# Attention products of a two-block transformer as plain float32 matmuls on halves of the array

## The chip, the core and the metric

The kernel runs on one core of a Trainium2 chip. TensorE multiplies matrices: a stationary operand of up to 128 rows by 128 columns is loaded, and a moving operand of up to 512 columns runs through it into a bank of PSUM. VectorE, ScalarE and GpSimd (POOL in the profile) do everything else, and SyncE starts the transfers from main memory. The metric is the device time of one execution in microseconds (us), as the median of several runs.

## What is computed

Two blocks of two layers each on 256 tokens of width 1024, all in float32. Each layer has a mixing part and a gated feed-forward part (FFN), and there is one FFN more ahead of the mixing part in the second block. The second block puts 16 meta tokens ahead of the 256. Cut to the attention parts, which are all that the change touches:

```python
def memory_cross_attention(q, mem_k, mem_v):              # 4 heads of 64, layers 0 and 1
    s = einsum("bshd,bmhd->bhsm", q, mem_k) * 64**-0.5
    return einsum("bhsm,bmhd->bshd", softmax(s), mem_v)

def stick_breaking_attention(q, k, v):                    # 12 heads of 64, layer 1
    z = einsum("bhtd,bhsd->bhts", qb, kb) * scale         # causal, blocks of 128 queries
    log_not = where(causal, log_sigmoid(-z), 0.0)
    a = where(causal, exp(log_sigmoid(z) + reverse_cumsum(log_not) - log_not), 0.0)
    out = einsum("bhts,bhsd->bhtd", a, vb)

def _diff_attention(...):                                 # 8 heads, each two maps of width 64, values of 128
    logits = einsum("bqhmd,bkhmd->bmhqk", qb, k) * scale + bias
    p = softmax(where(visible, logits, NEG_INF))
    out = einsum("bhqk,bkhe->bqhe", p[:, 0] - lam_full * p[:, 1], v)

def _dsa_attention(...):                                  # 16 heads over one latent of 256; 8 index heads of 64
    act = relu(einsum("bqhd,bsd->bqhs", qi, k_idx) * 64**-0.5)
    score = einsum("bqh,bqhs->bqs", wi, act)              # the 64 best keys of each query are kept
    logits = einsum("bqhr,bqkr->bqhk", qa, kv) * 256**-0.5 + bias
    o_lat = einsum("bqhk,bqkr->bqhr", softmax(logits), kv)
    out = einsum("bqhr,hrd->bqhd", o_lat, w_uv)
```

The kernel multiplies latent and `w_uv` first and so has values of width 64 per head in the last one.

## The kernel before

Activations lie feature by token: 8 tiles of 128 features by 256 (or, with the meta tokens, 272) tokens. Weights stream from main memory in pieces of 128 x 1024 words. Each piece is split in two on the way: ScalarE copies it to the shorter format float32r (`wh`, line 187), VectorE, for some pieces POOL, takes the difference (`wl`, line 189). Activations are split likewise by `split_act` and `split_scaled` (lines 216 to 223). A product of two split operands is three float32r matmuls, `mm3`: high by high, high by low, low by high (lines 212 to 214). The trace names these lines for nearly all of TensorE's work, in the attention as in the dense layers, so tiles tell the places apart: `z` and `s` are PSUM banks of scores, `o` of outputs, `mm` of dense products, `t`, `b` and `n` of transposes and norms.

The order of the work is not the code's. A scheduler reads the program, with the functions' calls as its order of preference, and moves instructions of each engine where data and buffers allow; it often puts the matmuls of one score between those of a dense product.

The stages in order of time: mix0 (gated convolution, and memory attention in `mem_pair`), FFN 0, mix1 (stick-breaking attention in `pair`, and `mem_pair`), FFNs 1 and 2, diff (`diff_mix`), FFNs 3 and 4, dsa (`dsa_mix`), FFN 5. How the attention parts use the array before:

- Scores with heads of 64 features (`mem_pair`, `pair`, the diff scores, dsa's index scores) have 64 rows of the array, the lower ones for even heads, the upper ones for odd heads; one head's three matmuls stand together in the code, with all 128 columns.
- Values for two heads of 64 (`mem_pair`, `pair`, dsa's `apply_v`) are loaded together as 128 columns, and each head's probabilities run through both. Half of what comes out is not used: `pair_out` picks rows 0 to 63 of the first head's 256 columns and rows 64 to 127 of the second's (line 551).
- In diff and dsa the probabilities of 256 queries over the keys are transposed by TensorE to four tiles of 128 columns (`probs_t`), split, and multiplied in four parts: 256 columns, 128 columns, and twice 128 columns for the meta positions, which have 48 rows only (`K = slice(0, 48)`, line 1027).
- dsa's scores have 256 features, two full tiles of rows (line 1229).
- dsa's search for the 64 best keys (`top_rounds`, 8 rounds on VectorE for each of two halves of the queries) follows the index scores; the first attention heads need its mask.

PSUM has eight banks. The kernel gives them to tags: `banks(mm=3, z=3, o=2)` in the first block and in all FFNs, other shares in diff and dsa.

Of the kernel before, what the change touches and what calls it, by code (L numbers as in the profile page):

```python
# [6 lines left out]
F32 = mybir.dt.float32  # L7
F32R = mybir.dt.float32r
# [21 lines left out]
HUGE = 3e38  # L30
TOPK = 64
# [99 lines left out]
class Net:  # L131
# [181 lines left out]
    def token_major(self, name, x, rc, dst):  # L313

        ws = [self.take(name, 4) for _ in range(2)]
        for tt in range(2):
# [5 lines left out]
            vh, vl = dst(tt)  # L322
            self.split_scaled(vh, vl, b[:, :S], rc[:, tt : tt + 1])
# [149 lines left out]
    def mem_side(self, i, mx, r_row, r_col, pk, tag):  # L473

        nc = self.nc
        kh = self.t(pk, [P, 2, S], tag + "kh", F32R)
        kl = self.t(pk, [P, 2, S], tag + "kl", F32R)
        banks = self.dense(f"mkv{i}", mx, S)
        for m in range(2):
            t = self.t(self.p_ev, [P, T], "ea")[:, :S]  # L480
            nc.vector.scalar_tensor_tensor(t, banks[m][:, :S], 0.125, r_row, ALU.mult, ALU.mult)
            self.split_act(kh[:, m], kl[:, m], t)
        self.ahead()
        vh = self.t(pk, [P, 2, S], tag + "vh", F32R)
        vl = self.t(pk, [P, 2, S], tag + "vl", F32R)
        self.token_major(f"mkv{i}", mx, r_col, lambda tt: (vh[:, tt], vl[:, tt]))
        self.ahead()
        return (kh, kl), (vh, vl)

    def pad_pairs(self, vh, vl, src, col, rows=P):  # L490

        s4 = src.rearrange("p (a e d) -> p a e d", e=2, d=64)
        for e in range(2):
            o = slice(192 * e, 192 * e + 64)
            if col is None:
                self.split_act(vh[:, :, o], vl[:, :, o], s4[:, :, e])
            else:
                self.split_scaled(vh[:, :, o], vl[:, :, o], s4[:, :, e], col)
# [8 lines left out]
    def mem_pair(self, qm, mk, mv, p, y, pt, nb=2):  # L507
# [3 lines left out]
        for e in range(2):  # L511
            rows = slice(e * 64, e * 64 + 64)
            s = self.bank("z")
# [21 lines left out]
            ph = self.t(pt, [P, 2, S], "th", F32R, bufs=nb)  # L535
            pl = self.t(pt, [P, 2, S], "tl", F32R, bufs=nb)
            self.split_act(ph, pl, b3)
# [889 lines left out]
```

## Time and profile before

| | |
|---|---|
| median of 3 runs | 1754.85 us (1753.32 to 1756.73) |
| profiled execution, its own time | 1751.51 us |
| its span, first to last instruction | 1749.8 us |
| TensorE busy | 1719.7 us, 13786 matmuls recorded |
| VectorE, ScalarE, POOL busy | 1165.5, 929.9, 435.5 us |
| mean granted clock of TensorE | 0.989 of full |

Busy time of an engine is the time in which at least one of its instructions runs. Matmuls are pipelined: one is recorded as running for some 0.28 us, while the next starts 0.12 us later. So the distance between two starts tells what a matmul takes of the queue, and the duration does not. Weight loads have records of their own (PEld) and run beside the matmuls. Where a row lists busy times by stretch, the order is TensorE, its weight loads, VectorE, ScalarE, POOL, with the number of instructions in brackets. The chain that ended last is followed back from the last instruction, at each step to what released it.

### The profile page before, as it was taken

To read this page: it belongs to the slowest core of one execution; us is meant where nothing else is said; L and a number is where in the kernel's file an instruction comes from. 1 tells how busy PE (TensorE), PEld (TensorE's weight loads), DVE (VectorE), ACT (ScalarE), POOL (GpSimd) and SP (SyncE) were. 2 spreads that over 40 slices of the span, in tenths; PEclk is the share of its full clock that TensorE was granted. 3 is DMA by queue.
4 is the path that set the end of the run, shared out by engine and by line. 5 is a ranking of instruction groups with operands and counts; after the bars stand their busy time and mean duration, and the time that the engine had idled before them with its cause. 6 is when DMAs were issued, how large, how long until landed. Compare 5 with 4: busy or idle time off the path is not lost.

```text
span 1749.8 us, 33756 instructions
## 1 busy us (share of the span) xinstructions
PE 1719.7 (98%) x13786; PEld 1687.2 (96%) x13786; DVE 1165.5 (67%) x1942; ACT 929.9 (53%) x1631; POOL 435.5 (25%) x450
## 2 busy tenths in 40 slices
PE   8999999999999999999999999999999989999999
PEld 7999999999999999999998999999999979999999
DVE  8867666677766666655978666556665587766653
ACT  6545445586544654444665544445444467655442
POOL 2023221013322022211443522111221234342210
PEclk9999999999999999999998999999999999999999
DMA  7456655423555545445531444444445433245552
GB/s 274 156 196 219 231 184 181 170 93 121 193 193 181 183 167 193 169 170 185 162 106 61 161 177 169 170 184 177 170 169 176 135 97 113 73 164 184 180 197 91
DMA packets 59931, 287.61 MB, mean 164 GB/s; under 512 B 12112, under 2 KB 22864, under 8 KB 29184
## 3 DMA queue, kind: packets, MB, share of 16 engines
q1 hardware_dynamic: 58944, 284.80, 46.6%
q8 instruction: 108, 1.77, 0.4%
q10 hardware_dynamic: 832, 0.66, 0.1%
q14 instruction: 47, 0.39, 0.1%
HBM read 284.34 MB, written 5.53 MB: 166 GB/s over the span
## 4 chain that ended last, share of the span: by engine, by line
PE 93%; DVE 5%; ACT 1%; DMA 1%; issue 0%; POOL 0%; ACTq 0%; DVEq 0%; POOLq 0%; SPq 0%
PE mm L212 21%; PE mm L214 21%; PE mm L213 21%; PE z L212 8%; PE z L213 8%; PE z L214 7%; DVE xl L223 1%; PE o L212 1%; PE o L213 1%; PE o L214 1%; PE s L212 1%; PE s L213 1%; PE s L214 1%; DMA X<-in_xT_dram 1%; DVE wl L189 1%
## 5 line engine op out<-in xcount | busy, mean ns | idle before, releaser
L187 ACT CAST wh<-raw 128x1024 fp32r<-128x1024 f32 (+1 forms) x526 | 541.7, 1032 | 606.8 <-PE mm L213 397.0
L189 DVE TENSOR_TENSOR wl<-raw,wh 128x1024 fp32r<-128x1024 f32 (+2 forms) x494 | 603.2, 1223 | 291.5 <-ACT wh L187 289.4
L212 PE MATMUL mm<-xh,wh 128*128 128x256 f32 (+1 forms) x1808 | 521.7, 289 | 1.5 <-DVE ea L703 0.6
L213 PE MATMUL mm<-xl,wh 128*128 128x256 f32 (+1 forms) x1808 | 518.1, 287 | 4.7 <-DVE xl L223 4.5
L214 PE MATMUL mm<-xh,wl 128*128 128x256 f32 (+1 forms) x1808 | 518.2, 287 | 0.0
L213 PEld LDWEIGHTS mm<-xl,wh 128*128 128x128 f32 x1808 | 341.4, 189 | 7.5 <-DVE xl L223 5.9
L212 PEld LDWEIGHTS mm<-xh,wh 128*128 128x128 f32 x1808 | 341.7, 189 | 5.0 <-DVE ea L703 0.9
L214 PEld LDWEIGHTS mm<-xh,wl 128*128 128x128 f32 x1808 | 342.0, 189 | 1.3 <-issue 0.2
L213 PE MATMUL z<-xl,wh 128*128 128x256 f32 (+1 forms) x1056 | 301.6, 286 | 1.5 <-DVE xl L223 1.3
L214 PE MATMUL z<-xh,wl 128*128 128x256 f32 (+1 forms) x1056 | 302.3, 286 | 0.0
L212 PE MATMUL z<-xh,wh 128*128 128x256 f32 (+1 forms) x1056 | 301.2, 285 | 0.0
L212 PE MATMUL mm<-gh,wh 128*128 128x256 f32 (+1 forms) x1056 | 300.5, 285 | 0.0
L214 PE MATMUL mm<-gh,wl 128*128 128x256 f32 (+1 forms) x1056 | 299.5, 284 | 0.0
L213 PE MATMUL mm<-gl,wh 128*128 128x256 f32 (+1 forms) x1056 | 299.5, 284 | 0.0
L339 POOL TENSOR_TENSOR es<-es,r 128x256 f32<-128x256 f32 (+1 forms) x110 | 152.3, 1387 | 466.8 <-ACT es L338 466.8
L213 PEld LDWEIGHTS z<-xl,wh 128*128 128x128 f32 x1056 | 199.2, 189 | 1.9 <-DVE xl L223 1.9
L214 PEld LDWEIGHTS z<-xh,wl 128*128 128x128 f32 x1056 | 199.8, 189 | 0.2
L212 PEld LDWEIGHTS z<-xh,wh 128*128 128x128 f32 x1056 | 199.5, 189 | 0.1
L213 PEld LDWEIGHTS mm<-gl,wh 128*128 128x128 f32 x1056 | 199.2, 189 | 0.0
L214 PEld LDWEIGHTS mm<-gh,wl 128*128 128x128 f32 x1056 | 198.5, 188 | 0.0
L212 PEld LDWEIGHTS mm<-gh,wh 128*128 128x128 f32 x1056 | 198.3, 188 | 0.0
L340 DVE TENSOR_TENSOR ea<-z,es 128x256 f32<-128x256 f32 (+1 forms) x132 | 57.1, 432 | 96.7 <-POOL es L339 48.9
(487 smaller groups left out, 2241.0 us busy)
## 6 DMA issues: line engine op xcount, KB each, us to landing
raw<-in_gu_dram SPq DMA_DIRECT2D x132, 1024.0 KB, 4.8
raw<-in_wd_dram SPq DMA_DIRECT2D x66, 1024.0 KB, 4.8
raw<-in_aw_dram SPq DMA_DIRECT2D x12, 1024.0 KB, 4.8
raw<-in_a_in_dram SPq DMA_DIRECT2D x9, 1024.0 KB, 4.9
raw<-in_wo_dram SPq DMA_DIRECT2D x12, 768.0 KB, 4.2
nb<-scr SPq DMA_DIRECT2D x32, 136.0 KB, 2.3
scr<-relrow SPq DMA_DIRECT2D x16, 271.5 KB, 5.4
raw<-in_mkv_dram SPq DMA_DIRECT2D x4, 1024.0 KB, 5.4
```

Of the source, the lines that this page charges most:

```text
L187: self.nc.scalar.copy(h[:, :c], t[:, x : x + c])
L189: eng.tensor_tensor(l[:, :c], t[:, x : x + c], h[:, :c].bitcast(F32), ALU.subtract)
L212: mm(out, wh, xh, start=first, stop=False, skip_group_check=chk)
L213: mm(out, wh, xl, start=False, stop=False, skip_group_check=chk)
L214: mm(out, wl, xh, start=False, stop=last, skip_group_check=chk)
L223: self.nc.vector.scalar_tensor_tensor(l, src, col, h.bitcast(F32), ALU.mult, ALU.subtract)
L339: nc.gpsimd.tensor_tensor(s, s, r, ALU.mult)
L340: nc.vector.tensor_tensor(a, B[:, :cols], s, ALU.mult)
```

## The change

All products inside the attention become plain float32 matmuls on unsplit operands. Queries, keys, values and probabilities are kept as one float32 tile each, so the copies to float32r become plain copies or go, and the subtractions on VectorE go. Products of dense layers, also those that make queries, keys and values, stay as they are.

Where a head has 64 features, a new helper `both` writes two heads turn by turn: the scores of one on the upper 64 rows of the array, of the other on the lower. Values of two heads are no longer loaded together: each head has 64 columns of the array, the two halves again turn by turn, and both outputs land in the same 256 columns of the bank, on rows 0 to 63 and 64 to 127; `pair_out` is one split instead of two. The meta positions' value tiles are filled with zeros to 128 rows. In mix1 the banks are shared out as mm=2, z=4, o=2. In dsa the value product is written once per two heads. In diff the norm's factor is multiplied in while queries and keys are scaled, on VectorE, instead of by POOL ahead.

```diff
+HALF = [slice(0, 64), slice(64, P)]
...
+    def both(self, jobs, start, stop):
+        for out, w, x in jobs[::-1]:
+            self.nc.tensor.matmul(out, w, x, start=start, stop=stop, skip_group_check=True)
...
@@ mem_pair @@
-            for tt in range(2):
-                c = slice(tt * P, (tt + 1) * P)
-                self.mm3(
-                    s[:, tt * S : (tt + 1) * S], (qm[0][rows, p, c], qm[1][rows, p, c]),
-                    (mk[0][rows, p], mk[1][rows, p]), True, True,
-                )
+        ss = [self.bank("z") for _ in range(2)]
+        for tt in range(2):
+            c = slice(tt * P, (tt + 1) * P)
+            self.both([(s[:, tt * S : (tt + 1) * S], qm[r, p, c], mk[r, p]) for s, r in zip(ss, HALF)], True, True)
...
-            self.split_act(ph, pl, b3)
+            nc.scalar.copy(pr, b3)
...
-                self.mm3(o[:, e * S : (e + 1) * S], v, (ph[:, kt], pl[:, kt]), kt == 0, kt == 1)
+            self.both([(o[r, :S], mv[:, kt, p * P + r.start : p * P + r.stop], pr[:, kt]) for r, pr in zip(HALF, ps)],
+                      kt == 0, kt == 1)
...
@@ pair_out @@
-        for e in range(2):
-            r = slice(64 * e, 64 * e + 64)
-            self.split_act(y[0][r, k, :S], y[1][r, k, :S], o[r, e * S : (e + 1) * S])
+        self.split_act(y[0][:, k, :S], y[1][:, k, :S], o[:, :S])
...
@@ block1_mix1 @@
+        self.banks(mm=2, z=4, o=2)
...
+                zs = [self.bank("z") for _ in range(2)]
+                self.both([(z[:, :S], k[r, p, :P], q[r]) for z, r in zip(zs, HALF)], True, False)
+                self.both([(z[:, S:NC], k[r, p, P:], q[r, P:]) for z, r in zip(zs, HALF)], False, False)
...
-                    self.split_act(ah, al, av)
...
+                self.both([(o[r, :S], v[:, 0, p, r], av[:, :S]) for r, av in zip(HALF, avs)], True, False)
+                self.both([(o[r, P:S], v[:, 1, p, r], av[:, S:]) for r, av in zip(HALF, avs)], False, True)
...
@@ diff_mix @@
+            vm = self.t(p1, [P, NH, P], "vm")
+            vn = [self.t(p1, [P, P], f"vn{i}") for i in range(LAG + 1)]
...
-                nc.gpsimd.tensor_tensor(x, x, u, ALU.mult)
...
-                    self.split_scaled(qk[0][:, i, P:], qk[1][:, i, P:], x[:, i], g)
+                    nc.vector.scalar_tensor_tensor(qk[:, i, P:], x[:, i], g, u[:, i], ALU.mult, ALU.mult)
...
+                for qc, k0, n, c, tt in SEGS:
+                    self.both([(s[:, c], qk[r, 0, P + NM + qc.start : P + NM + qc.stop], qk[r, 1, k0 : k0 + n])
+                               for s, r in zip(ss, HALF)], True, True)
...
-                self.apply_v(os[0], e, (ph, pl), lambda i: tuple(v[:, i] for v in vr),
-                             tuple(v[:, h] for v in vm), vq)
+                for i, (oc, pc, v) in enumerate(self.v_parts(vr, vm[:, h], vq)):
+                    nc.tensor.matmul(os[0][:, e * S + oc.start : e * S + oc.stop], v, pr[:, pc],
+                                     start=e == 0 and i == 0, stop=e == 1 and i == 3, skip_group_check=True)
...
@@ dsa_mix @@
-                self.split_act(qi[0][:, m], qi[1][:, m], b[:, :S])
+                nc.scalar.copy(qi[:, m], b[:, :S])
...
-                        self.mm3(s[:, c], (q[0][:, k, qc], q[1][:, k, qc]),
-                                 (ckg[0][:, k, k0 : k0 + n], ckg[1][:, k, k0 : k0 + n]), k == 0, k == 1)
+                        nc.tensor.matmul(s[:, c], q[:, k, qc], ckg[:, k, k0 : k0 + n], start=k == 0, stop=k == 1)
...
+                    for n, two_ in enumerate(zip(*parts)):
+                        self.both([(o[r, oc], w, ps[i][:, pc]) for i, (r, (oc, pc, w)) in enumerate(zip(HALF, two_))],
+                                  n == 0, n == 3)
```

On TensorE, in dsa, the value product of a second head. Before, a head's four parts are three matmuls each; `v0h` and `v0l` are the halves of the values, `ph` and `pl` of the probabilities, and the last number is output rows x columns. The first row is the end of a dense product, then come the parts of 256 and of 128 columns:

```order
L214 MATMUL mm_17462<-wh_17168,ckvl_16675 48x256
L212 MATMUL o_17431<-ph_17552,v0h_17085 128x256
L213 MATMUL o_17431<-pl_17553,v0h_17085 128x256
L214 MATMUL o_17431<-ph_17552,v0l_17086 128x256
L212 MATMUL o_17431<-ph_17552,v0h_17085 128x128
L213 MATMUL o_17431<-pl_17553,v0h_17085 128x128
L214 MATMUL o_17431<-ph_17552,v0l_17086 128x128
```

The next six rows are two more such threes, on 48 rows of the array. After, the same place for both heads of the pair, `pr_16989` and `pr_16924` their probabilities:

```order
L1179 MATMUL s_17042<-ckg_16080,q_16732 128x272 x2
L222 MATMUL o_16991<-pr_16989,v_2357_16444 64x256
L222 MATMUL o_16991<-pr_16924,v_2357_16444 64x256
L222 MATMUL o_16991<-pr_16989,v_2357_16444 64x128
L222 MATMUL o_16991<-pr_16924,v_2357_16444 64x128
```

Two more pairs of 64x128 follow. The two heads' products stand turn by turn, each on 64 columns, and nothing on 48 rows stands among them.

On TensorE, in diff, before: one head's value product behind the last row of the next head's scores (`s`, on 64 rows). The last six rows, `vmh` to `vn1l`, are on 48 rows, and the row behind them is a transpose on all rows:

```order
L214 MATMUL s_10778<-qkh_10508,qkl_10509 16x16
L213 MATMUL o_10403<-pl_10604,vh_10551 128x256
L214 MATMUL o_10403<-ph_10603,vl_10552 128x256
L212 MATMUL o_10403<-ph_10603,vh_10551 128x128
L213 MATMUL o_10403<-pl_10604,vh_10551 128x128
L214 MATMUL o_10403<-ph_10603,vl_10552 128x128
L212 MATMUL o_10403<-ph_10603,vmh_10084 128x128
L213 MATMUL o_10403<-pl_10604,vmh_10084 128x128
L214 MATMUL o_10403<-ph_10603,vml_10085 128x128
L212 MATMUL o_10403<-ph_10603,vn1h_10088 128x128
L213 MATMUL o_10403<-pl_10604,vn1h_10088 128x128
L214 MATMUL o_10403<-ph_10603,vn1l_10089 128x128
```

After, the same product of another head, with a norm's product behind it:

```order
L918 MATMUL o_10408<-pr_10579,v_10543 128x256
L918 MATMUL o_10408<-pr_10579,v_10543 128x128
L918 MATMUL o_10408<-pr_10579,vm_9764 128x128
L918 MATMUL o_10408<-pr_10579,vn_1375_9765 128x128
L849 MATMUL n_10678<-sq_10674,blk 128x272
```

Before, the rows in use change ahead of the product, within it and behind it; after, all of the product is on 128 rows, and so is what stands around it. Twelve rows have become four.

## Rows read from the trace of the kernel before

**Rows 1.** From the page: the span, the engines' busy times, the chain's shares.
```profile
span 1749.8 us, 33756 instructions
...
PE 1719.7 (98%) x13786; PEld 1687.2 (96%) x13786; DVE 1165.5 (67%) x1942; ACT 929.9 (53%) x1631; POOL 435.5 (25%) x450
...
PE 93%; DVE 5%; ACT 1%; DMA 1%; issue 0%; POOL 0%; ACTq 0%; DVEq 0%; POOLq 0%; SPq 0%
```

**Rows 2.** Busy by stage: stretch, length, engines' busy us, PE clock, DMA share, GB/s.
```profile
14.00:125.50 111.50, 110.90 (x925) 108.85 (x924) 86.56 (x150) 63.11 (x108) 15.19 (x14) 1.00 0.55 192
...
317.00:432.00 115.00, 113.33 (x942) 109.63 (x941) 83.48 (x152) 83.61 (x167) 17.91 (x28) 1.00 0.36 124
...
822.00:986.00 164.00, 161.77 (x1145) 147.38 (x1143) 131.49 (x308) 99.12 (x231) 74.03 (x88) 0.94 0.38 122
...
1390.00:1553.00 163.00, 154.32 (x1199) 146.87 (x1198) 129.13 (x357) 105.52 (x302) 62.10 (x92) 0.96 0.34 106
```

**Rows 3.** Chain in order of time (start, us, what), at 316 and 843.
```profile
316.34 0.12 PE mm L214
316.45 0.43 PE o L279 x2
...
843.33 0.92 PE n L880 x4
844.24 0.13 PE mm L212
```

**Rows 4.** Groups by form on TensorE (count | busy us, mean ns): line 880.
```profile
L880 PE MATMUL n<-sq,blk 128*128 128x272 f32 x32 | 10.2, 417 | 0.0
```

**Rows 5.** Timeline of TensorE (start, us, tile, rows*columns used, moving operand) at 1418.
```profile
1418.25 0.23 PE L212 MATMUL s<-kih,qih 64*128 64x144 f32 x1
1418.32 0.27 PE L213 MATMUL s<-kil,qih 64*128 64x144 f32 x1
1418.43 0.27 PE L214 MATMUL s<-kih,qil 64*128 64x144 f32 x1
1418.63 0.38 PE L212 MATMUL mm<-wh,cqh 128*128 128x256 f32 x1
1418.85 0.28 PE L213 MATMUL mm<-wl,cqh 128*128 128x256 f32 x1
```

**Rows 6.** Timeline of TensorE at 906: 128-column products of the meta positions.
```profile
906.28 0.27 PE L214 MATMUL o<-ph,vml 48*128 48x128 f32 x1
906.39 0.27 PE L212 MATMUL o<-ph,vn0h 48*128 48x128 f32 x1
```

**Rows 7.** Timeline of TensorE at 1411: from 8 columns of the array to 128.
```profile
1411.08 0.28 PE L214 MATMUL mm<-xh,wl 128*8 128x256 f32 x1
1411.20 0.28 PE L212 MATMUL mm<-cqh,wh 128*128 128x256 f32 x1
```

**Rows 8.** Timeline of TensorE at 1415: two heads' index scores, one per half.
```profile
1415.72 0.24 PE L212 MATMUL s<-kih,qih 64*128 64x144 f32 x2
1415.79 0.28 PE L213 MATMUL s<-kil,qih 64*128 64x144 f32 x2
1415.90 0.29 PE L214 MATMUL s<-kih,qil 64*128 64x144 f32 x2
1416.03 0.33 PE L212 MATMUL o<-kih,qih 64*128 64x272 f32 x1
```

**Rows 9.** Busy by stretch, columns as in rows 2: diff and dsa.
```profile
902.00:922.00 20.00, 20.00 (x124) 17.60 (x124) 13.62 (x33) 11.33 (x26) 9.77 (x12) 0.83 0.33 101
1428.00:1445.00 17.00, 12.93 (x73) 12.00 (x74) 16.97 (x73) 10.15 (x33) 7.30 (x14) 0.73 0.22 68
```

**Rows 10.** Groups by form on VectorE from 1411 to 1445: splits of the index queries.
```profile
L219 DVE TENSOR_TENSOR qil<-mm,qih 128x256 fp32r<-128x256 f32 x4 | 1.7, 416 | 0.0
```

**Rows 11.** Groups by form on VectorE, whole span: weight splits, evacuation of queries.
```profile
L189 DVE TENSOR_TENSOR wl<-raw,wh 128x1024 fp32r<-128x1024 f32 x465 | 575.6, 1240 | 282.4 <-ACT wh L187 280.9 <-issue 0.2
...
L555 DVE TENSOR_TENSOR ea<-mm,r 128x256 f32<-128x256 f32 x10 | 4.2, 421 | 4.0 <-PE mm L214 3.8
```

More of the change, by code (lines that the diff above doesn't have):

```diff
@@ L510, in mem_pair @@
         ps = []
[L511 to L519 removed]
+        ss = [self.bank("z") for _ in range(2)]
+        for tt in range(2):
+            c = slice(tt * P, (tt + 1) * P)
+            self.both([(s[:, tt * S : (tt + 1) * S], qm[r, p, c], mk[r, p]) for s, r in zip(ss, HALF)], True, True)
+        for s in ss:
             s3 = s.rearrange("p (a b) -> p a b", a=2)
@@ L589, in block1_mix0 @@
             for m in range(2):
-                self.q_evac(qh[:, m], ql[:, m], banks[m], r)
+                self.q_evac(qm[:, m], banks[m], r)
             self.ahead()
@@ L736, in block1_mix1 @@
         self.memctx.close()
+        self.banks(mm=3, z=3, o=2)
     def mask_diag(self, t):
@@ L919, in attend @@
                 pm = []
-                for m in range(2):
-                    rows = slice(m * 64, m * 64 + 64)
-                    s = self.bank("s")
-                    q = lambda c: tuple(x[rows, 0, P + c.start : P + c.stop] for x in qk)
-                    k = lambda c0, n: tuple(x[rows, 1, c0 : c0 + n] for x in qk)
-                    for qc, k0, n, c, tt in SEGS:
-                        self.mm3(s[:, c], q(slice(qc.start + NM, qc.stop + NM)), k(k0, n), True, True)
-                    self.mm3(s[:NM, W : W + NM], q(slice(0, NM)), k(P, NM), True, True)
+                ss = [self.bank("s") for _ in range(2)]
+                for qc, k0, n, c, tt in SEGS:
+                    self.both([(s[:, c], qk[r, 0, P + NM + qc.start : P + NM + qc.stop], qk[r, 1, k0 : k0 + n])
+                               for s, r in zip(ss, HALF)], True, True)
+                self.both([(s[:NM, W : W + NM], qk[r, 0, P : P + NM], qk[r, 1, P : P + NM]) for s, r in zip(ss, HALF)],
+                          True, True)
+                for m, s in enumerate(ss):
                     L, nb = Ls[h % 2][m], nbs[m]
@@ L991, in meta @@
                     c = slice(h * NM, (h + 1) * NM)
-                    self.mm3(o[:, c], tuple(v[:NM, h0 + h] for v in vm), (ph[:, c], pl[:, c]), True, True)
+                    nc.tensor.matmul(o[:, c], vm[:NM, h0 + h], ph[:, c], start=True, stop=True)
                 sub_norm(o, y[0][:, h0:h1, :NM], y[1][:, h0:h1, :NM], n, NM, "n", None)
@@ L1150, in top_rounds @@
                         nc.vector.match_replace(wk[:, c], m8, src[:, c], -HUGE)
-            vs = [tuple(self.t(p1, [P, 4, S], f"v{i}{c}", F32R) for c in "hl") for i in range(2)]
-            for v in vs[0] + vs[1]:
-                nc.gpsimd.memset(v[:48, 2:].bitcast(F32), 0.0)
+            vs = [self.t(p1, [P, 4, S], f"v{i}") for i in range(2)]
+            for v in vs:
+                nc.gpsimd.memset(v[:, 2:], 0.0)
             def values(g):
@@ L1217, in mask @@
                     nc.gpsimd.tensor_tensor(nb[:, c], nb[:, c], msk[:, c], ALU.add)
-            os = {}
+            ps = {}
             def attend(h):
```

199 lines of the change are left out of this document (70 added, 129 removed).

## The prediction

> **What bounds the kernel now.** I read the page first. TensorE is busy for 98% of the span and holds 93% of the chain that ended last [rows 1], so a change that takes 0.6 us off TensorE's queue should show nearly all of it, as long as no other engine becomes late. Then the busy times by stage [rows 2]: the four attention stages are mix0 (14 to 125.5), mix1 (317 to 432), diff (822 to 986) and dsa (1390 to 1553). TensorE is busy for 98 to 99% of the first three and 95% of dsa. VectorE is at 78, 73, 80 and 79% there, ScalarE at 73% at most. A busy TensorE is not yet a TensorE that moves columns, so I priced its instructions by the distance between starts, not by their durations.
>
> **Prices.** One rounded-operand (float32r) matmul of 256 columns starts 0.12 us after the one before; a plain float32 matmul of 256 columns takes 0.43, one of 272 columns 0.46 (the row x4 holds two of them), a float32r one of 272 some 0.125 [rows 3]. Each plain matmul leaves two records: line 880 runs 16 times and has x32 [rows 4]; so a record is 0.215 or 0.23. A float32r matmul of 144 columns needs 0.11, hardly less than one of 256 [rows 5], and so does one of 128 columns [rows 6]: below 256 columns something other than columns sets the pace. Plain matmuls of 128 and 144 columns are not in the trace. Two bounds: twice 0.11, since each is two records, and 0.43 and 0.46 cut by columns, 0.215 and 0.245. These are close; as estimates I take 0.22 and 0.245.
>
> So three split products against one plain one: 0.36 against 0.43 at 256 columns, 0.375 against 0.46 at 272, but 0.33 against 0.22 and 0.245 at 128 and 144. The Trainium skill (FP8 and Floating Point Precision, TensorE Precision Notes) says that true float32 takes four passes through the array; that speaks against this change, four passes for three, a third more. The rows for 256 and 272 columns show about a fifth more.
>
> **Two further prices.** A move between matmuls that use all 128 rows of the array and ones that use 64: the 144-column product on 64 rows at 1418.43 is followed by a full one 0.20 later instead of 0.11, and that one by its next 0.22 later instead of 0.12 [rows 5]. That is 0.19 us per change of rows, each way. A change of columns costs nothing: from 8 columns of the array to 128 the step stays at 0.12 [rows 7]. The Trainium skill (TensorEngine Tiling, Key Properties) states that changing the tiling mode, not just the tile, drains the engine. For rows the trace agrees (0.19), for these columns it does not.
>
> Second, halves work at the same time: in dsa's index scores two heads stand turn by turn, one on each half of the rows, and six 144-column products are through in 1415.72 to 1416.03, 0.31 us [rows 8]; the three of one head alone need about as much, 0.29 to 0.31 [rows 5].
>
> **The change, part by part.** A plain product in halves is two records on one half, then two on the other, and starts keep their order. The first half's second record can run beside the second half's first, no more. With u for a record, one pair of heads takes 3u instead of 4u, two pairs in a row 5u instead of 8u, four 9u instead of 16u; unequal widths are worked the same way. Counted from the code, before, then after alone, then overlapped:
> Memory attention, 4 times: 24 x 0.12 = 2.88; 8 x 0.43 = 3.44; 2.15.
> Stick-breaking pair, 6 times: 12 x 0.12 + 12 x 0.11 = 2.76; 4 x 0.43 + 4 x 0.22 = 2.60; 1.73.
> diff scores, 8 times: 6 x 0.125 + 6 x 0.11 = 1.41; 2 x 0.46 + 2 x 0.245 = 1.41; 0.94 (the 16-column ones are left out).
> diff values, 8 times, all columns in use, no halves: 3 x 0.12 + 9 x 0.11 = 1.35; 0.43 + 3 x 0.22 = 1.09.
> dsa index scores, 4 pairs: 1.41 and 1.41. The built order tears most of these pairs apart, so I count no overlap.
> dsa scores, 16 times, full rows: 1.41 and 1.41.
> dsa values, 8 pairs: 2.70; 2.18; 1.29.
> Alone this is 4 x 0.56 - 6 x 0.16 - 8 x 0.26 - 8 x 0.52 = 5 us less. Overlapped it is 4 x 0.73 + 6 x 1.03 + 8 x 0.47 + 8 x 0.26 + 8 x 1.41 = 26 us less. Two corrections. In mix1 the built order tears the score pairs of both memory heads and of one stick-breaking pair apart, which is 2 us. And before has overlap too: by the starts some 40 products run beside a partner as in [rows 8], up to 0.11 each, 4 us. **Products: 20 us less**, between 1 (no overlap, 5 - 4) and 32 (every pair fully side by side).
>
> Changes of rows: in the built order before has 159 (8, 26, 78 and 47 in the four stages), after 66 (8, 18, 30 and 10). The 48-row products of the 16 meta positions go: their tiles are filled with zeros to 128 rows. 93 x 0.19 = **18 us less**. The bounds are 0, if the drains hide in waits, and 18; TensorE hardly waits in diff, so I stay near the upper end and take 2 off for drains in stretches where it waits. The change brings some 53 changes to and from halves of columns. By [rows 7] they cost nothing; by the row price 10 us.
>
> VectorE: the low halves go. That matters only where VectorE is late, in dsa's top-64 search: from 1428 to 1445 it is busy for 16.97 of 17 us and TensorE for 12.93 [rows 9]. Ahead of it four splits of the index queries (1.7) [rows 10] and one of the keys go: 2 us less. Elsewhere VectorE's and ScalarE's share is cover, and it grows. diff's new scale-by-norm on VectorE takes the place of the split it drops.
>
> What the change could cost: mix1 gets four z banks and two mm banks instead of three. A product group lasts 24 x 0.12 = 2.9 us, its evacuation 0.42 on VectorE, perhaps behind a 1.24 us weight split [rows 11]: hidden; 3 us if it is not. dsa's value product now waits for both heads of a pair; only the pair's write to y stands behind it, which nothing reads before the output projection. At nothing.
>
> Clock: from 902 to 922 the granted clock is 0.83 of full, from 1428 to 1445 0.73 [rows 9]; it is 1.00 over mix0 and mix1 [rows 2]. 0.17 of 20 us is a fall to 1.2 GHz for 7 us, 3.4 us lost, behind a stretch of 64-row and 48-row products. Such stretches get shorter and fewer, but the work per head too: I take 0, with 3.4 either way for each fall.
>
> **Sum.** -20 - 18 + 2 - 2 = -38 us. The profiled execution took 1751.5 (its span is 1749.8 [rows 1]): 1713.5. The median of the runs, 1754.85, is 3.3 above it, so I say **1717**. Its own range is 1709 to 1727: two falls of the clock fewer, or two more and the banks.
>
> **Rivals.** (1) Column halves don't run side by side; no row of before shows such a pair. Then 4 x 0.65 + 6 x 0.43 + 8 x 0.89 = 12 us come back: 1729. The Trainium skill (TensorE: Matmul & The Clock Gate, The mechanism) lets a weight load pass a running matmul only where the row groups differ; column halves share them. (2) No half runs beside another, because the two records of a plain matmul block the queue: 19 us come back (20 - 1), 1736. Against it stand [rows 8], for float32r. (3) Column changes drain like rows, 53 x 0.19: 1727. By the rule of the Trainium skill in Key Properties, named above, this is what would happen. (4) Full overlap, 12 us more, and two falls of the clock fewer: 1698.
> (5) Slower: each turn from half to half drains. 208 half products at 0.19 are 40 us on top of (2): 1776. It decides from 100 drains on; [rows 8] speak against it for rows, nothing for columns or for plain operands. (6) The clock falls once per head or pair: 8 + 8 falls at 3.4 are 54 us, 1771; from 12 falls on the gain is gone. For it: falls stand just where half-array work stands. Against: mix1 has such work and no fall.
> (7) A plain product costs a third more than its three split ones at every width. All split products are about 100 us by the counts above; 33 us more, 4 of old overlap lost, the changes of rows won: 1754.85 + 33 + 4 - 18 + 2 - 2 = 1774. Against it speak [rows 5, 6], since narrow split products pay for three starts. This is the four-pass rule of the Trainium skill, named above, taken alone.
> (8) The change doesn't do what it says, as the scheduler tears every pair apart: that is (2), 1736. In the built order it is the exception.
>
> **Chances.** Forecast 0.55; (1) 0.12; (2) 0.11; (3) 0.06; (4) 0.07; (5) 0.04; (6) 0.02, (7) 0.02; about no change 0.01. A measurement of this kernel tells 0.2%, 3.5 us, from no change. Faster 0.91, same 0.02, slower 0.07. The range 1700 to 1738 takes in (1) to (3) and leaves out (4) to (7).
>
> **What would show it.** Right: TensorE's stretch in diff shorter by about 12 us and in dsa by about 18, mix1 by 7, mix0 by 1, the other stages unchanged; two halves' records within 0.02 us of each other in mix1's scores and dsa's values; no step of 0.20 around the value products. Wrong: records of a pair 0.22 apart four times in a row; a step of 0.2 at each column half; granted clock below 0.9 over diff or dsa; TensorE waiting for mm banks in mix1.

## The result

The changed kernel takes 1725.95 us (median of 4 runs, 1724.67 to 1729.42) where the kernel before took 1755.79 in the runs beside it: a ratio of 0.9835, 95% interval 0.9816 to 0.9854. That is 30 us less by the medians and 27 by the two profiled executions (1751.51 and 1724.67). Forecast were 38 less, 1717; the range of 1700 to 1738 holds the time. One run of the kernel before took 4186 us and is left out of every comparison below.

Part of the gain is TensorE's clock. Each run has its span and its mean granted clock; the span times what is missing to 1 is an estimate of what the clock cost it. Over the 31 runs of the kernel before that stand beside the experiments it is 20 us on average (granted clock 0.988), over the 8 runs of the changed kernel 16 (0.991). So some 5 us of the gain are clock, and some 22 are work and waits.

The page of the changed kernel, the lines that answer to [rows 1]:

```profile
span 1722.9 us, 32907 instructions
...
PE 1682.0 (98%) x13474; PEld 1638.4 (95%) x13474; DVE 1095.4 (64%) x1789; ACT 898.6 (52%) x1559; POOL 417.9 (24%) x426
...
PE 93%; DVE 3%; ACT 1%; issue 1%; DMA 1%; POOL 0%; ACTq 0%; DVEq 0%; POOLq 0%
```

Busy by stage in the changed kernel, columns as in [rows 2]; each stretch now ends where the next FFN's products begin:

```profile
14.00:126.50 112.50, 111.90 (x917) 107.94 (x916) 80.05 (x134) 61.03 (x101) 15.61 (x14) 0.99 0.56 191
318.00:434.80 116.80, 110.71 (x890) 101.82 (x888) 70.91 (x116) 71.45 (x138) 24.22 (x31) 1.00 0.37 127
824.70:970.00 145.30, 137.74 (x1011) 125.12 (x1010) 113.81 (x270) 87.16 (x210) 56.90 (x78) 0.98 0.42 134
1380.60:1528.40 147.80, 133.81 (x1050) 120.87 (x1048) 103.29 (x304) 101.53 (x293) 62.87 (x87) 0.97 0.39 119
```

Measured from one stage's opening norm sums to the next stage's (each attention stage with the FFN behind it, so that no boundary is a matter of taste), the time moved by +0.8 us in mix0, +0.8 in mix1, -12.4 in diff and -16.1 in dsa; the two FFNs that stand alone moved by 0.1. Expected were -1, -7, -12 and -18. So most of the 11 us that are missing, 7.8, are missing in mix1. Yet TensorE is less busy there than in [rows 2], though the stretch is cut 1.8 us longer: what was won came back as idle time, 6.1 us in this stretch.

**Where TensorE's time went.** For every trace I added up the distances between starts on TensorE, each put to the product that began it (told by its tiles). A distance over 0.36 us (0.33 for projections) counts as 0.13 of work, the rest as a wait; time at half clock counts half, the other half is the row "clock". Attention products carry their changes of rows and columns. Some records are missing from any trace, so a row is good to some tenths; between waits and other work the limits can move a microsecond or two, and only their sum is firm. The columns are experiments of the next section: zero128 is "changes of rows alone", fullcols "halves of columns undone", rowseq "halves of rows undone", nopool the changed kernel with splits moved off GpSimd, all_three "all together". Each column is one execution.

```
us                     before  zero128   after  fullcols  rowseq  nopool  all_three
memory, stick-breaking   27.8     27.8    20.9      26.6    21.6    20.9       20.4
diff scores              15.2     15.2     9.6       9.6    17.0     9.6        9.7
diff values, meta        16.7     15.1    11.0      11.1    10.9    10.9       11.0
dsa and index scores     29.0     29.2    25.9      25.4    26.2    25.6       25.7
dsa values               25.3     21.4     9.9      17.6     9.9     9.9        9.9
attention, sum          114.0    108.7    77.3      90.3    85.6    76.9       76.7
all other work         1577.5   1576.5  1579.8    1578.4  1580.9  1581.2     1578.5
waits                    30.1     30.7    41.5      39.2    36.6    36.6       39.4
clock                    19.8     18.6    16.9      18.5    15.4    11.8       10.6
```

From before to after: attention products with their changes 36.7 less, other work 2.3 more (the projection that follows a change pays for it), waits 11.4 more, clock 2.9 less. That is -25.9 of the 26.8 between the two profiled executions. The products with their changes gave what was forecast for them in sum; 11 us came back in waits.

The changed kernel's waits on TensorE (waited for: us in total, times, longest), the six largest of those that begin after the loads:

```profile
PE n L1160 <- ACT qx L1154: 5.6, 1, 5.6
PE mm L214 <- ACT xh L226: 4.7, 3, 3.8
PE mm L214 <- DVE X L390: 4.2, 3, 2.3
PE mm L214 <- ACT wh L189: 3.7, 1, 3.7
PE o L222 <- ACT pr L984: 2.0, 2, 1.4
PE mm L214 <- DVE k L674: 1.8, 1, 1.8
```

The same view of the kernel before:

```profile
PE n L1203 <- ACT qx L1197: 4.9, 1, 4.9
PE mm L213 <- DVE xl L223: 4.5, 4, 1.3
PE n L1203 <- DVE qx L1199: 1.4, 1, 1.4
```

The first line, dsa's top-64 search, was there before. The next three are the three places where an attention stage hands over: the last pair of diff (3.8 of L226), the end of mix1's output projection (L390), the start of dsa's FFN (L189). The kernel before waited at two of them too, but less: the 4.5 us of its second line are four waits for splits of X, two behind diff and two at dsa's FFN, and the view has none at FFN1's start. The fifth is the value product that waits for both heads, the sixth mix1's first product group behind the new bank split.

### The profile page after: what moved, and what is told of

Its sections match the earlier page's. It is cut to its first block, busy times and chain, and to the rows that moved or that the text cites. A ratio compares the mean times of both kernels' runs of the same rounds, so it can differ in the third digit from the quotient of the medians.

```text
span 1722.9 us, 32907 instructions
## 1 busy us (share of the span) xinstructions
PE 1682.0 (98%) x13474; PEld 1638.4 (95%) x13474; DVE 1095.4 (64%) x1789; ACT 898.6 (52%) x1559; POOL 417.9 (24%) x426
## 4 chain that ended last, share of the span: by engine, by line
PE 93%; DVE 3%; ACT 1%; issue 1%; DMA 1%; SPq 0%; POOL 0%; ACTq 0%; DVEq 0%; POOLq 0%
PE mm L214 21%; PE mm L215 21%; PE mm L216 21%; PE z L216 7%; PE z L215 7%; PE z L214 7%; DVE xl L231 1%; PE s L1179 1%; PE o L222 1%; PE z L222 1%; DMA X<-in_xT_dram 1%; PE s L222 1%; PE o L918 0%; PE n L849 0%; DVE X L390 0%
## 5 line engine op out<-in xcount | busy, mean ns | idle before, releaser
L189 ACT CAST wh<-raw 128x1024 fp32r<-128x1024 f32 (+1 forms) x526 | 541.9, 1032 | 622.9 <-PE mm L215 409.7
```

Source lines behind the costliest of these rows:

```text
L189: self.nc.scalar.copy(h[:, :c], t[:, x : x + c])
```

## Experiments

**The changed kernel again,** as the measure for three others.

> The changed kernel once more, unchanged, as the measure for the three others of this group. All theories: 1724 to 1729 us, ratio to the kernel before 0.9835. Its trace is asked one thing: whether the granted clock falls at the same work as in the first trace of the changed kernel (3.4 us near 435, three of 3.4 us in the differential stage, 6.8 us near 1414 and near 1527) or elsewhere. The same places: the clock's share of the gain belongs to the kernel. Other places: it is chance of one execution.

1724.1 us, ratio 0.9843 (0.9821 to 0.9865). The clock falls stand at the same work as before, near 435, 936, 943, 970, 1414 and 1527; only one in the first 15 us did not come back. The waits of over 1 us are the same ones, within 0.1 us. So the places are the kernel's own. How much the clock costs is not fixed: over the kernel's runs the mean granted clock goes from 0.989 to 0.992, and 0.003 of the span is 5 us.

**Banks in mix1,** three ways.

```diff
-        self.banks(mm=2, z=4, o=2)
+        self.banks(mm=3, z=4, o=1)
```

> Changed kernel, with three mm banks, four z and one o in mix1 instead of 2, 4, 2. Theory (banks): mix1 won its 7 us in the products and gave them back in waits for an mm bank (starts 2.07 apart at 324, 1.63 at 427.7, 2.58 at 432.3 in the trace of the changed kernel) and in the clock fall of 3.4 us right behind the last (1.7 us). Then 4 to 7 us less than the changed kernel, 1718 to 1722. Rival (torn pairs): mix1 gained nothing since its score pairs stand apart, and banks are not what ends last: within 2 us of the changed kernel. Rival (one o bank): the next pair's transposes wait for the bank of the last, 2 to 4 us more than the changed kernel.

1721.0 us, 0.9822 (0.9799 to 0.9845).

```diff
-        self.banks(mm=2, z=4, o=2)
...
-        self.banks(mm=3, z=3, o=2)
```

> Changed kernel with the bank split of the kernel before in mix1 (three mm, three z, two o, no change of pools). Theory (banks): the waits for mm banks go, 4 to 7 us, but two score tiles at once from three z banks make a pair wait for the one before, up to 0.5 us for each of 8 pairs: between 0 and 7 us less than the changed kernel, likeliest 3. Rival (torn pairs): no change, within 2 us. If it is slower than the changed kernel, four z banks were needed and the split was right.

1723.31 us, 0.9835 (0.9815 to 0.9855).

```diff
-            self.out_proj(1, y, S, Xr)
+            self.out_proj(1, y, S, Xr, ("mm", "z"))
```

> Changed kernel with two mm banks kept in mix1, but the second pass of its output projection takes mm and z banks in turn. Theory (banks): the waits at 427.7 and 432.3 (1.4 and 2.3 us) and the clock fall behind them (1.7) go, the one at 324 stays: 3 to 5.5 us less than the changed kernel. Rival (torn pairs, or the start of the FFN waits for VectorE's additions whatever bank they come from): within 1.5 us of the changed kernel, and the gap before the first FFN product stays over 2 us.

1721.29 us, 0.9824 (0.9803 to 0.9846). Three microseconds less for the first and the third are at the low end of what was expected and no more than the spread of the runs, so the traces have to carry the reading. With a third mm bank the wait for k (L674) is gone, waits of 0.5 to 0.9 come at 397, where memory attention's transposes and values now share one o bank, and the wait at the hand-over to FFN1 stays at 2.5 us. With mm and z in turn it is 2.0. With z=3 the k wait is 0.6, and the waits at the hand-over are gone altogether: the built order there has the attention's last value products at 429.7 instead of 420.3, and so has less of the projection behind them. But waits of 0.7 and 0.9 stand inside the attention, and the stick-breaking scores take 8.0 us in place of 5.6, since more pairs are torn (137 alternations of halves in the built order in place of 149). So the third mm bank by itself is worth some 2 us, the wait for k, not 4 to 7; the wait at the hand-over goes or stays with the built order.

**Prices by themselves:** patterns of 8 or 16 matmuls in program order, nothing else on TensorE but 32 full float32r products ahead of each.

> No part of the network is left but loading x: the output is not the reference's. TensorE runs patterns of 8 to 16 matmuls, each behind 32 full-array float32r ones of 256 columns, in program order, each pattern under its own tile name. Expected distances between starts by the prediction's prices: full float32r 0.12; full plain 0.43 for 256 columns, 0.245 for 144, 0.22 for 128. Halves of the rows or columns turn by turn: theory (record by record) a pair of plain 256-column products in 0.43 to 0.45; the prediction's in-order rule gives 0.65 for a pair alone and 0.43 to 0.54 each for a chain; no overlap gives 0.86. The same half twice: 0.43 each. Full array against 64 rows in turn: 0.12 + 0.19 at each step. Full against 64 columns: theory (a half of columns drains as rows do) 0.31 each step for float32r and 0.62 for plain; rival (only plain ones drain) 0.12 and 0.62; rival (the prediction: columns are free) 0.12 and 0.43. Full against 48 and 8 columns: 0.12, as in the kernel before.

Timeline of TensorE in that kernel (start, us from the first start to the last end, tile; 16 records in each):

```profile
13.12 2.08 PE L456 MATMUL fullr<-h 128*128 128x256 f32 x16
18.88 3.62 PE L456 MATMUL fullp<-f 128*128 128x256 f32 x16
26.17 2.12 PE L456 MATMUL fullpn<-f 128*128 128x144 f32 x16
...
37.67 3.72 PE L456 MATMUL rowsame<-f 64*128 64x256 f32 x16
45.34 2.00 PE L456 MATMUL rowpair<-f 64*128 64x256 f32 x16
...
56.48 3.67 PE L456 MATMUL colsame<-f 128*64 128x256 f32 x16
64.11 1.95 PE L456 MATMUL colpair<-f 128*64 128x256 f32 x16
...
80.16 4.97 PE L456 MATMUL fullrow<-h 128*128 128x256 f32 x16
89.00 2.03 PE L456 MATMUL fullcol<-h 128*128 128x256 f32 x16
94.69 4.79 PE L456 MATMUL fullcolp<-f 128*128 128x256 f32 x16
103.34 4.99 PE L456 MATMUL fullrowp<-f 128*128 128x256 f32 x16
```

fullr is 16 float32r products, fullp 8 plain ones of two records; the estimate of 0.245 for 144 columns is confirmed by fullpn (8 in 2.12). rowpair and colpair are the two halves turn by turn, rowsame and colsame the same half eight times: turn by turn takes half as long, on rows and on columns alike, and the starts of a pair stand 0.007 us apart, record by record. That is better than the prediction's rule (3 records' time for a pair, measured 2). fullrow has the full array and 64 rows in turn: (4.97 - 2.08) / 15 changes = 0.19 each, as in [rows 5]. fullcol is the same with 64 columns, float32r: 2.03, nothing. fullcolp with plain operands: (4.79 - 3.62) / 7 changes = 0.17 each. So columns are free for float32r, as [rows 7] showed, and not for plain operands, which [rows 7] could not show. The rule on changes of the tiling mode (the Trainium skill, TensorEngine Tiling, Key Properties) holds for the plain ones.

**Changes of rows alone:** the kernel before, split operands and all, with its 48-row tiles filled up to 128 rows.

```diff
-        K = slice(0, 48)
+        K = slice(0, P)
```

> The kernel before, with split operands as they were, only the tiles of the 16 meta positions filled with zeros to 128 rows, in the differential and the sparse stage, and used whole. Its built order has 109 changes of rows instead of 159. The prediction's price, 0.19 each: 50 x 0.19 = 9.5 us less than before, 1746 (ratio 0.9946). Rival (the drains hide in waits or in the 0.11 floor of narrow products): 0 to 3 us less. Rival (the clock): full rows instead of 48 keep the clock up, and the falls of 20 us in the differential stage go: 5 to 10 us more, 15 to 19 less in all.

1743.47 us against 1751.69, ratio 0.9957 (0.994 to 0.9973): 7.5 us less by the ratio, for 50 changes fewer 0.15 each, but with what the clock gave. In the table the two value rows give 5.5 of it, other work 1, clock 1.2; waits are 0.6 more. So without the clock a change is worth 0.13 here, two thirds of the price. Over all runs the clock gave more, some 4 us (granted clock 0.991 against 0.989), so 0.13 is rather too much than too little. Changes of rows cost time in the kernel, little of it hid in waits, but 0.19 for each was too high: the result lies between the price and the rival.

**Halves of columns undone:** each head's value product on all 128 columns (here the stick-breaking pair; memory and dsa likewise).

```diff
-                self.both([(o[r, :S], v[:, 0, p, r], av[:, :S]) for r, av in zip(HALF, avs)], True, False)
-                self.both([(o[r, P:S], v[:, 1, p, r], av[:, S:]) for r, av in zip(HALF, avs)], False, True)
+                for e, av in enumerate(avs):
+                    self.both([(o[:, e * S : (e + 1) * S], v[:, 0, p], av[:, :S])], e == 0, False)
+                    self.both([(o[:, e * S + P : (e + 1) * S], v[:, 1, p], av[:, S:])], False, e == 1)
```

> Changed kernel, but the value products of memory, stick-breaking and sparse attention use all 128 columns for each head and keep half of what comes out: no halves of columns, so no side by side there and no changes to 64 columns. By the trace of the changed kernel these products take 6.8 us in mix1 and 10.6 in the sparse stage with their drains. Alone they would take 6 x 1.30 + 2 x 1.72 = 11.2 in mix1 and 8 x 2.18 = 17.4 in the sparse stage, 3.4 in place of about 2 in mix0. Theory (side by side, drains of 0.19 already in): 4.4 + 6.8 + 1.4 = 12 to 13 us more than the changed kernel, 1737 to 1740. Rival (the drains eat what the halves win): 0 to 4 us more. Each head's product could start without the other's here: that could take 1 to 2 us back.

1734.25 us, 0.9903 (0.9886 to 0.992): 10 to 11 us more than the changed kernel (0.9843 and 0.9835). The table has 13 us more of products (7.7 in dsa's values, 5.7 in the first block) and 2.3 less of waits. Side by side on columns is real and worth more than its drains.

**Halves of rows undone:** scores written head after head (here the stick-breaking pair; memory, diff and index scores likewise).

```diff
-                self.both([(z[:, :S], k[r, p, :P], q[r]) for z, r in zip(zs, HALF)], True, False)
-                self.both([(z[:, S:NC], k[r, p, P:], q[r, P:]) for z, r in zip(zs, HALF)], False, False)
+                for z, r in zip(zs, HALF):
+                    self.both([(z[:, :S], k[r, p, :P], q[r])], True, False)
+                    self.both([(z[:, S:NC], k[r, p, P:], q[r, P:])], False, False)
```

> Changed kernel, but the score products of the two heads of a pair are written head after head instead of turn by turn (memory, stick-breaking, differential and index scores); columns stay as they are. Counted from the built order 102 alternations of halves instead of 149, 80 changes of rows instead of 66. Theory (record by record): what the differential scores won by halves goes, 8 x (1.41 - 1.11) = 2.4 us, index scores 1.5, stick-breaking 6 x 0.4 = 2.4, and 14 x 0.19 = 2.7 of changes: 6 to 9 us more than the changed kernel. Rival (the end of one head's products runs beside the start of the other's anyway, and the first head's softmax starts earlier): 0 to 3 us more.

1726.98 us, 0.9865 (0.9847 to 0.9883): 4 to 5 us more, between theory and rival. TensorE has 8.3 us more of attention products (7.4 of them in diff's scores, where the 16-column products now stand between the heads and bring changes of their own; 2.4 were expected there), and waits 4.9 less. That looks as if TensorE would have waited for more than half of what it was given to do, but it does not show that: the one wait of 3.8 us at diff's hand-over is not there in this kernel, whose built order is another one at that place (below).

**What TensorE waits for at the hand-overs.** In diff it is the norm of the last two heads. VectorE in the changed kernel, and GpSimd beside it:

```profile
962.96 2.88 DVE L264 SCALAR_TENSOR_TENSOR onr<-onr,onr 128x512 f32<-128x512 f32 x1
...
966.12 2.49 DVE L265 SCALAR_TENSOR_TENSOR osq<-onr,onr 128x512 f32<-128x512 f32 x1
```

```profile
962.89 5.16 POOL L191 TENSOR_TENSOR wl<-raw,wh 128x1024 fp32r<-128x1024 f32 x2 [6.22 <-ACT wh L189]
```

The same steps in the kernel before:

```profile
974.17 0.69 DVE L256 SCALAR_TENSOR_TENSOR onr<-onr,onr 128x512 f32<-128x512 f32 x1
...
975.13 0.68 DVE L257 SCALAR_TENSOR_TENSOR osq<-onr,onr 128x512 f32<-128x512 f32 x1
```

```profile
977.66 7.59 POOL L189 TENSOR_TENSOR wl<-raw,wh 128x1024 fp32r<-128x1024 f32 x3 [5.04 <-ACT wh L187]
```

And TensorE in the changed kernel, behind its last product of the first pass at 966.05:

```profile
970.09 0.39 PE L214 MATMUL mm<-xh,wh 128*128 128x272 f32 x1 [3.75 <-ACT xh L226]
```

Before, GpSimd's splits of FFN weights came after the norm; now they run beside it, and two steps of 0.69 take 2.88 and 2.49. The same at FFN1's start, where two splits of X that take 0.50 each elsewhere take 2.94 together while GpSimd runs a split from 430.86 to 433.25, and TensorE waits until 434.87 for the addition behind them. The Trainium skill (SBUF — State Buffer, SBUF: two separate sides) has VectorE and GpSimd share one port pair under an exclusive lock, also for VectorE operations with two SBUF inputs; these rows agree. So the next edit moves those splits to VectorE: twelve, four for each of three FFNs (the text on record says eight at first, and twelve further on).

```diff
-ON_POOL |= {(f"gu{i}", j, m) for i in (0, 1, 3, 5) for j in range(2) for m in range(2)}
+ON_POOL |= {(f"gu{i}", j, m) for i in (0,) for j in range(2) for m in range(2)}
```

> Changed kernel, with the eight low halves of first FFN weights that GpSimd makes behind mix1, diff and dsa (two of 1024 columns from each of two loads, for three FFNs) made on VectorE instead. Theory (joints): by the trace of the changed kernel TensorE waits 3.9 us at 966 for the last two heads of diff; on that chain two VectorE steps of 128x512 take 2.88 and 2.49 us while two GpSimd splits run (962.9 to 968), and the same steps took 0.69 and 0.68 in the kernel before, where GpSimd's splits came after them. So the wait at 966 shrinks by 3 to 4 us; at the starts of FFN1 and FFN5, where splits of X take 1.6 to 2.5 us instead of 0.52, by 1 to 2 each; VectorE gets 12 splits of 1.22 more there: 3 to 7 us less than the changed kernel in all. Rival (VectorE's own queue sets the joints): the 12 splits stand before the chain instead, 0 to 4 us more.

1719.05 us, 0.9805 (0.9789 to 0.9822): 5 to 7 us less than the changed kernel (0.9843 and 0.9835). VectorE on the same chain in that kernel:

```profile
957.05 0.68 DVE L264 SCALAR_TENSOR_TENSOR onr<-onr,onr 128x512 f32<-128x512 f32 x1
...
958.79 0.69 DVE L265 SCALAR_TENSOR_TENSOR osq<-onr,onr 128x512 f32<-128x512 f32 x1
```

The wait at 966 fell from 3.9 to under 0.5, that at FFN1's start from 2.5 to 0.7; at dsa's FFN, where 1 to 2 less were expected, 3.6 us stayed, so there GpSimd's splits are not what it waits for. The two clock falls that stood right behind the first two waits are gone too in this execution. It is the fastest of five (1715.11 us, granted clock 0.994); three of the five took 1719 to 1720 at 0.991 or 0.992, so the clock of this column in the table is better than the typical one. The same edit in the kernel before:

> The same edit in the kernel before, which waits 0.4, 2.8 and 2.8 us at the same three places. Theory (joints: the change brought TensorE there earlier, and only then GpSimd's splits fall on the chain that it waits for): 0 to 3 us less than before, fewer than the changed kernel gains. Rival (the splits on GpSimd cost both kernels the same): as much as the changed kernel gains.

1759.1 us, 1.0033 (1.0021 to 1.0045): 6 us **more**. Neither theory nor rival said so; in its trace waits are 5.1 us more and the clock 5.6. Its steps on the chain are 0.69 as ever, but three weight splits of 1.22 now stand between them where two stood, and TensorE waits 3.6 us at that place:

```profile
PE mm L212 <- ACT xh L218: 3.6, 1, 3.6
```

What else differs is the built order. Between the last norm sums of diff and the first product of the output projection's second pass in the s bank, the traces have this many product records on mm: 83 in the kernel before, 57 with its GpSimd splits moved, 58 in the changed kernel, 78 with its splits moved. The chain takes 8 to 12 us from norm sums to the split y; 57 or 58 records are 8 us of cover, 78 or 83 are 11. A wait follows wherever the cover is the short one. In the changed kernel the edit changed both, the chain and the cover.

Other runs help to tell them apart, though none was made for it. All leave the splits on GpSimd. With halves of rows undone the cover is 72 records, GpSimd's splits start behind the norm's steps, which take 0.68 each, and the longest wait at that place is 0.3 us. With banks 3, 3, 2 in mix1 the cover is 78 records, as with the splits moved, and the splits run beside the split of y, the end of the chain:

```profile
963.99 7.54 POOL L191 TENSOR_TENSOR wl<-raw,wh 128x1024 fp32r<-128x1024 f32 x3 [6.33 <-ACT wh L189]
```

```profile
966.46 2.81 DVE L227 TENSOR_TENSOR xl<-osq,xh 128x512 fp32r<-128x512 f32 x1 [1.09 <-ACT xh L226]
```

```profile
PE mm L215 <- DVE xl L227: 1.8, 1, 1.8
```

With the splits moved and the same 78 records, that step takes 0.68 and no wait there is over 0.3 us. The other three runs with the splits on GpSimd (halves of columns undone, banks 3, 4, 1, mm and z in turn) have 57 records and wait 3.7 or 3.8 us. So at this hand-over GpSimd's splits alone cost some 2 us where the cover is long; where it is short TensorE waits 3.6 to 3.8 us with them or without. The cover that the built order leaves decides more than GpSimd does. Why the scheduler leaves 57 records in one kernel and 78 in another is not shown.

**All together.**

> Changed kernel with both edits: three mm banks, four z, one o in mix1 (3 us less alone), and no FFN splits on GpSimd behind the attention stages. Theory: the waits lie at different places and the gains add, 1714 to 1719. Rival (one gain hides the other, since both shorten the wait at FFN1's start): 1719 to 1721.

1719.98 us, 0.981 (0.9792 to 0.9828): no better than the GpSimd edit alone, as the rival had it. At FFN1's start TensorE waits 1.9 us again, with a clock fall behind it, although no split is on GpSimd there:

```profile
PE mm L214 <- DVE X L390: 2.4, 2, 1.9
```

VectorE has one of the moved weight splits (1.21 us at 427.29) ahead of the additions to X that TensorE waits for. So the 0.7 us above were not the edit's alone.

> As the one before, and the second pass of mix1's output projection takes mm and z banks in turn (2.8 us less alone). Theory: that pass waited for VectorE's additions in whatever bank once mm has three, so at most 1.5 us less than without: 1713 to 1718. Rival (banks still): 2 to 3 us less.

1714.37 us (1713.57 to 1715.47), 0.9782 (0.9766 to 0.9797). This is the fastest of all, some 10 us under the changed kernel. It is 5.6 us under the run before it, more than theory (1.5) or rival (2 to 3) allowed. Its gain over the changed kernel is 6.3 us of clock and 2.1 of waits in the table; it has no fall at FFN1 and none behind diff. Compared with the GpSimd edit alone it is mostly clock that makes it faster: all its runs have a granted clock of 0.993 or 0.994, and the profiled execution of the GpSimd edit, at 0.994 too, has the same span of 1713.4 us.

```profile
span 1713.4 us, 32895 instructions
...
PE 1678.3 (98%) x13474; PEld 1634.5 (95%) x13474; DVE 1101.0 (64%) x1801; ACT 898.4 (52%) x1559; POOL 393.8 (23%) x414
```

## Why the prediction was right, and where not

**Products and changes of rows: right in the sum, by luck, as errors cancel.** 20 + 18 = 38 us were forecast, 36.7 measured, 2.3 of them paid back by the projections next to a change. By parts, with their changes: first block 6.9 less, diff 11.3, dsa 18.5. Three steps were wrong. The halves run side by side record by record, so the upper bound of the products (32 us, "every pair fully side by side") was nearer than the 20 of the in-order rule. One row of the changed kernel shows a whole pair of stick-breaking values, and two torn pairs of memory scores ahead of it (timeline of TensorE):

```profile
383.12 1.13 PE L222 MATMUL z<-m1k,qm 64*128 64x256 f32 x4
...
384.85 1.13 PE L222 MATMUL z<-m1k,qm 64*128 64x256 f32 x4
385.91 0.87 PE L222 MATMUL o<-av,v 128*64 128x256 f32 x8
386.71 0.38 PE L657 MATMUL z<-th,cstr 128*128 128x256 f32 x1
```

Four records of one head alone, of 256 columns each, take 1.06 us to the next start; eight records of two heads, half of them of 256 and half of 128 columns, take 0.80. The second step was the zero for changes of columns. The trace of the changed kernel has 36 changes to and from 64 columns, not the 53 that the prediction counted; at 0.17 they are 6 us. The zero was read from [rows 7], a float32r product on 8 columns, and carried over to plain ones on 64; the bound by the row price was in the text and would have been nearer. The third step was the row price. The torn score pairs of mix1 were foreseen: memory scores 6.2 before, 6.4 after.

**Widths: right.** dsa's scores, plain at full rows with no halves, take 22.3 us in place of 23.4; forecast was no change. The estimates for 128 and 144 columns held.

**Row price: right alone, too high in the kernel.** It is 0.19 by itself, and at most 0.13 without the clock in the run that changes nothing else. By that, the 93 changes are worth 12 us at most, not 18.

**VectorE in dsa's top-64 search: too much.** Forecast were 2 us less; the waits there went from 4.7 and 1.6 to 4.6 and 0.4, 1.3 less.

**The step that failed is "at nothing" for what is late next.** The sum had 2 us for hidden drains, nothing for the banks (3 if not hidden) and nothing for the value product that waits for both heads. Waits rose by 11.4 us: 4.9 in mix1 and at its FFN's start, 4.0 in diff and behind it, 2.4 in dsa and behind it, 1 at the kernel's start, and 1 less in short ones. Banks were about 2 of it, inside the bound given, and the value product that waits for both heads 2. Most of the rest is a term that the sum did not have: the hand-overs, where TensorE has output projection to do while a chain on VectorE, ScalarE and GpSimd finishes. At diff's, the new built order left 8 us of it instead of 11 and put GpSimd's splits beside the chain. That the waits stand there is shown; what made the built order is not. That TensorE "is busy for 98 to 99%" of the first three stages, from [rows 2], was an average; the end of each attention stage had to be read by itself.

**Clock: within its bound, and in the forecast's favour.** 0 was taken; it was 2.9 us less in the profiled execution, 4.6 in the second, some 5 over all runs. Without these the time would lie that much further from the forecast. Inside diff, falls of 20 us became falls of 7 ([rows 9] had one of them); new ones of 3.4 came behind the waits at FFN1's start and behind diff. The windows view has the one at FFN1, right behind the wait that ends at 434.87:

```profile
430.00:434.80 4.80, 2.58 (x21) 2.37 (x19) 4.47 (x8) 3.17 (x6) 3.86 (x3) 1.00 0.24 61
434.90:438.30 3.40, 3.40 (x17) 3.40 (x18) 3.40 (x5) 1.60 (x4) 1.74 (x3) 0.53 0.65 270
```

**Rivals.** (1), (2) and (8) fell by the records and by the two runs without halves; (3) was true of plain operands, for 36 changes; (4) was true of the overlap, and its 1698 failed by the waits; (5) fell, a turn between halves costs nothing; (6) fell, there is no fall per head; (7), the four passes, fell by dsa's scores.

## What to carry to other kernels

When a change takes work off the engine that bounds the kernel, go to each place where a stage hands over and count what that engine still has to do while the other engines' chain finishes; part of the gain can come back there as waits (here waits took 11 of 38 us in all). A small edit elsewhere can make a new built order and move such a wait, so look at the place again in every trace. Two plain float32 products on opposite halves of the array's rows or columns cost what one costs, if they stand next to each other in the built order, and each stretch of them costs two changes, 0.17 to 0.19 us each by themselves and, for rows, 0.13 at most in the kernel before. An elementwise step on GpSimd is not free while VectorE has a chain to finish (2.88 us for a step of 0.69).

## What the runs showed of the hardware

- Two halves of the array run side by side record by record, 0.003 to 0.007 us apart, for plain operands on rows and on columns and for float32r on rows; eight plain products, four on each half of the rows, take about half the time of eight on one half (2.00 against 3.72 us).
- A change between 128 and 64 columns is free for float32r (16 take 2.03 us with a change at each, 2.08 without) and costs 0.17 us for plain operands. Changes of rows cost 0.19 for both. All this holds for the kernel of patterns, one execution.
- A VectorE step with two SBUF inputs took 2.88 us in place of 0.69 while GpSimd ran an elementwise operation on SBUF.
- In the kernel of patterns, the granted clock fell to half in the middle of 128 rows and 48 rows in turn, with nothing waited for; the six patterns ahead of it that put the full array and a part of it in turn ran at 1.00. The windows view of it:

```profile
80.16:84.90 4.74, 4.74 (x18) 2.80 (x16) 0.00 (x0) 0.00 (x0) 0.00 (x0) 1.00 0.00 0
...
127.00:134.00 7.00, 7.00 (x28) 5.97 (x28) 0.00 (x0) 0.00 (x0) 0.00 (x0) 0.53 0.00 0
```

Open is why TensorE still waits 3.5 us at the start of dsa's FFN in the fastest kernel; its product there waits for an addition to X that VectorE reaches late, and no run on the changed kernel brought that wait much under 3 us.
